# A hybrid decoder block whose down projection is computed as seven block products

## The chip, the cores and the metric

One core of a Trainium2 chip runs one launch of the kernel. The metric is the device time of that launch in microseconds (us), the median over several runs. TensorE (PE) multiplies matrices, VectorE (DVE) and ScalarE (ACT) work elementwise, GpSimd (POOL) does small elementwise work, SyncE (SP) begins the transfers. A copy engine's transfer is called a DMA here.

## What is computed

A decoder block on a sequence of 1024 tokens and 1024 channels, all float32: a Mamba-2 state scan and a differential attention side by side, merged by gates, then a gated feed-forward layer with a short causal convolution. The part that matters is the last one:

```python
u = causal_dwconv(h2 @ w_up[layer], conv_ffn_w[layer], conv_ffn_b[layer])
u_gate, u_val = jnp.split(u, 2, axis=-1)
f = (jax.nn.gelu(u_gate, approximate=True) * u_val) @ w_down[layer]
x = x + g2 * rms_norm(f, post_norm2_w[layer])
```

`w_up` is 1024 x 5632, `w_down` 2816 x 1024. The first projections of the block (`xbc` for the scan, then `z` with `dt`) and the scan itself matter too, since the change puts work beside them.

## The kernel before

Every matrix product is done on PE in a split form: each float32 operand is cut into a high and a low part (`split`: a copy on ACT for the high part, a subtraction on DVE for the low one, lines 80 to 82), and three products are summed, high x high, high x low, low x high. So one block of 128 x 128 against 512 columns costs three matmuls.

The stages in order: a first stage that normalizes x, with the first blocks of xbc and of a gate; xbc (12 blocks, with sums over rows of `w_ada` on DVE beside it); z (three column ranges of 8 token tiles each); the state scan, in which GpSimd multiplies and adds (lines 615, 616, 652, 653) and PE follows an order written by hand; q, k and gates; attention; the output products; the mix with `w_out`; up; down.

**Up** (lines 1219 to 1334) runs 22 turns over blocks of 128 channels, `fb` from 0 to 21. A turn computes a gate block and a value block together as a 2 x 2 block product in Strassen's scheme (Winograd's form): seven products instead of eight, each of 4 x 3 matmuls of 128 x 512, 84 matmuls in a turn. `order` names them: b11, b21, t2, t1, t3, b22, t4, where the right operands are blocks of h2 or sums of them. The left operands are blocks of `w_up` or sums s1 to s4 that DVE forms (line 1310). Each left operand is split into one of 12 buffers that go round (`hl_tile`): four slots of their own (`hls`) and the eight split buffers `whi` and `wlo`, which all weights share. Raw blocks of weights pass through three buffers (`wraw`). The products are accumulated in PSUM banks X, Z and Y; ACT and DVE take them out (lines 1305, 1306, 1313 to 1321) into `cg` and `cv`. X is used by four of the seven products, so that t4, for example, waits until DVE has formed `cv` from t3's sum (line 1317). Then ACT and DVE do the convolution, the gelu and the product into `ug` (lines 1325 to 1329), and SP stores `ug` to `gd` in HBM.

**Down** (lines 1336 to 1390) runs two halves of 512 tokens. For each half it loads and splits the 22 blocks of `gd` (line 1352), then runs two column halves (accumulators fx and fy). In each it loads `w_down` two blocks at a time (line 94), splits them, and does for 4 token tiles 3 matmuls per block: 2 x 2 x 22 x 4 x 3 = 1056 in all. ACT sums squares, DVE multiplies by `g2r`; after the second column half come the root (GpSimd, line 130), the scaling with the residual (line 1389) and the store.

Large tiles lie in 43 slots of 4 KB per partition (`Slots`), handed out from the front of a free list and put back at its end; all 43 are in use during up. A new tile in a slot waits until the last tile there has been read. Except in blocks under `manual_schedule`, a scheduler sets the order of each engine's instructions by its own model of when operands are ready, so an instruction may be put well ahead of its place in the text; each engine then runs its list strictly in order. Up, down and the loop over z are ordered by it; in xbc only PE's order is by hand.

Of the kernel before, what the change touches and what calls it, by code (L numbers as in the profile page):

```python
# [17 lines left out]
P = 128  # L18
# [16 lines left out]
class Slots:  # L35
# [18 lines left out]
def kernel(ctx: ExitStack, tc: tile.TileContext, a: dict, out: bass.AP, dbg=None):  # L54
# [55 lines left out]
    def new_hl(name):  # L110
        return SL.get(name, F32R, (P, 2, HALF))
# [218 lines left out]
    gd = [dp.tile([P, S], F32, tag=f"gd{i}", name=f"gd{i}") for i in range(NFF)]  # L330
# [55 lines left out]
    brow = SL.get("brow")  # L386
    n_ada, rows_done = 0, 0
# [4 lines left out]
    with tc.manual_schedule(engines={EN.PE}):  # L392
        for b in range(12):
# [46 lines left out]
    n_ev = 0  # L440
# [17 lines left out]
    SL.put(*ev)  # L458
# [761 lines left out]
    hls = [SL.get(f"hls{i}") for i in range(4)]  # L1220
# [36 lines left out]
    for fb in range(2):  # L1257
        up_first(fb)
# [35 lines left out]
    for fb in range(NFF):  # L1294
        cg, cv = cgv[fb % 2]
        e1, e2 = evs[fb % 2][:, 0, :], evs[fb % 2][:, 1, :]
        if fb >= 2:
            up_first(fb)
# [23 lines left out]
        g_ = ug[fb % 2]  # L1322
# [7 lines left out]
        SP.dma_start(gd[fb], g_)  # L1330
    SL.put(*sab, *hls, *cgv[0], *cgv[1], *evs)
    for n, _ in order:
        SL.put(*HB[n])
    SL.put(*ug, uv)

    g2r = SL.get("g2r")
    SP.dma_start(g2r, rowd[3].broadcast_to([P, D]))
    fo = [SL.get(f"fo{i}") for i in range(4)]
    x1r = [SL.get(f"x1r{i}") for i in range(4)]
    tf = SL.get("tf", F32, (P, HALF))  # L1340
    gst = [SL.get(f"gst{i}", F32, (P, 2, HALF)) for i in range(2)]
    gT = None
    ssf = const("ssf", [P, 8, 2])
    rsf = const("rsf", [P, 8])
    for half in range(2):
        if half == 1:
            SL.put(*gT)
        gT = [None] * NFF
        for fb in range(NFF):
            gT[fb] = new_hl(f"g{half}_{fb}")  # L1350
            st = gst[fb // 2 % 2][:, fb % 2, :]
            SP.dma_start(st, gd[fb][:, half * HALF : (half + 1) * HALF])
            split(gT[fb][:, 0, :], gT[fb][:, 1, :], st)
        for ch in range(2):
            if ch == 0:
                acs = [ps_wa(f"fx{half}_0"), ps_wa(f"fx{half}_1"), ps_wb(f"fx{half}_2"), ps_wc(f"fx{half}_3")]
            else:
                mmx = [ps_mm(f"fy{half}_{i}") for i in range(2)]
                acs = [mmx[i // 2][:, i % 2, :] for i in range(4)]
            last = half == 1 and ch == 1  # L1360
            wd = {}
            sched = []
            for kp in range(NFF // 2):
                if not last or kp < NFF // 2 - 3:
                    sched += [(kp, q) for q in range(4)]
            if last:
                sched += [(kp, q) for q in range(4) for kp in range(NFF // 2 - 3, NFF // 2)]
            for kp, q in sched:
                if kp not in wd:
                    wd[kp] = load_moving(a["w_down"], 2 * kp, 2, ch * HALF, HALF, f"wd{half}_{ch}_{kp}")  # L1370
                tsl = slice(q * P, (q + 1) * P)
                for kk in range(2):
                    k = 2 * kp + kk
                    wh, wl = wd[kp][0][:, kk, :], wd[kp][1][:, kk, :]
                    T.matmul(acs[q], gT[k][:, 0, tsl], wh, start=(k == 0), stop=False)  # L1375
                    T.matmul(acs[q], gT[k][:, 0, tsl], wl, start=False, stop=False)  # L1376
                    T.matmul(acs[q], gT[k][:, 1, tsl], wh, start=False, stop=(k == NFF - 1))  # L1377
            csl = slice(ch * HALF, (ch + 1) * HALF)
            for q in range(4):
                i = 4 * half + q  # L1380
                A.activation(tf, acs[q], AF.Square, accum_out=ssf[:, i, ch : ch + 1])
                V.tensor_tensor(fo[q][:, csl], acs[q], g2r[:, csl], op=ALU.mult)
                if ch == 0:
                    SP.dma_start(x1r[q], x1d[i])
                    continue
                r_ = rsf[:, i : i + 1]
                V.tensor_tensor(r_, ssf[:, i, 0:1], ssf[:, i, 1:2], op=ALU.add)
                rstd_of(r_, r_, 1.0 / D, 1e-6)
                V.scalar_tensor_tensor(fo[q], fo[q], r_, x1r[q], op0=ALU.mult, op1=ALU.add)
                SP.dma_start(out[i * P : (i + 1) * P, :], fo[q])  # L1390
# [65 lines left out]
```

## Time and profile before

| | us |
|---|---|
| median of 3 runs (1977.42 to 1981.37) | 1979.33 |
| the profiled execution, its own time | 1979.32 |
| its span | 1977.5 |

The profile records one execution. Times in it count from the start of its span. An engine's busy time is the union of its instructions; PE's matmuls overlap each other, so that the duration of one is longer than the distance to the next. A group of instructions is named by line, engine, operation, and output <- inputs, with a count, the total and mean duration, and the idle time just before them with what ended it. In a row of waits, the instruction on the left waited for the one on the right: total us, times, longest. Some records can be missing from a trace (a few per cent). The rows themselves stand in the prediction.

In the order of time the stages lie about here: first stage to 75 us, xbc to 219, z to 308, scan to 480, q, k and output of the scan to 740, attention to 1067, output and mix to 1278, up to some 1730 (down begins inside its last turn, at 1717), down to the end.

### The profile page before, as it was taken

The page shows a single profiled execution, that of the slowest core. Times are in us where ns is not written, and L with a number is a line of the kernel's source. Part 1 is how long each engine was busy: PE and PEld are TensorE (multiplying, and loading weights), DVE is VectorE, ACT ScalarE, POOL GpSimd, SP SyncE. Part 2 cuts the span into 40 slices and gives each one's busy share as a digit, 9 for nine tenths or more (in the row PEclk, how much of TensorE's full clock was granted, in tenths as well). Part 3 has the DMA queues.
Part 4 walks back from the last instruction along what each step waited for, and adds up shares of the span by engine and source line. Part 5 has one row for each costly group of instructions (what it writes and reads, how often), then busy time and mean ns, then how long its engine had stood idle before and what let it go on. Part 6 is the DMA issues. An engine that isn't in the chain of part 4 may idle for free.

```text
span 1977.5 us, 24442 instructions
## 1 busy us (share of the span) xinstructions
PE 1905.0 (96%) x9260; PEld 1579.5 (80%) x9260; DVE 1167.4 (59%) x1782; ACT 834.7 (42%) x1606; POOL 117.0 (6%) x114
## 2 busy tenths in 40 slices
PE   6999999999999999999999999979999999999997
PEld 4787998878888788888887887758888888788886
DVE  6967334565172247767666445599787777664322
ACT  5532225554232135655556322366454554543221
POOL 0000002542010000000000000000000000000000
PEclk9999999999999999999999999989999999999999
DMA  9834232235337636565623552212222222574531
GB/s 303 297 117 161 78 108 79 91 107 177 117 75 226 220 106 177 154 168 147 183 89 136 182 185 107 93 50 100 96 75 86 84 77 86 175 245 144 181 97 63
DMA packets 120414, 269.06 MB, mean 136 GB/s; under 512 B 13284, under 2 KB 44644, under 8 KB 120296
## 3 DMA queue, kind: packets, MB, share of 16 engines
q1 hardware_dynamic: 120296, 267.50, 42.5%
q8 instruction: 73, 1.20, 0.2%
q14 instruction: 45, 0.37, 0.1%
HBM read 201.37 MB, written 66.08 MB: 135 GB/s over the span
## 4 chain that ended last, share of the span: by engine, by line
PE 85%; DVE 5%; DMA 4%; ACT 3%; SPq 1%; issue 1%; POOL 0%; POOLq 0%; ACTq 0%; DVEq 0%
PE up L1247 5%; PE up L1248 5%; PE up L1249 5%; PE o L1026 3%; PE fy L1377 2%; PE fy L1376 2%; PE fy L1375 2%; PE fx L1377 2%; PE fx L1376 2%; PE fx L1375 2%; PE upy L1249 2%; PE upy L1247 2%; PE upy L1248 2%; PE xbc L103 2%; PE xbc L105 2%; PE xbc L104 2%
## 5 line engine op out<-in xcount | busy, mean ns | idle before, releaser
L1247 PE MATMUL up<-t,wu_t 128*128 128x512 f32 x264 | 107.1, 406 | 4.4 <-DVE cg L1306 3.5
L82 DVE TENSOR_TENSOR wd_lo<-wd_raw,wd_hi 128x1024 fp32r<-128x1024 f32 x44 | 53.8, 1225 | 96.6 <-ACT wd_hi L81 94.8
L1248 PE MATMUL up<-t,wu_t 128*128 128x512 f32 x264 | 104.0, 394 | 0.0
L1249 PE MATMUL up<-t,wu_t 128*128 128x512 f32 x264 | 103.4, 392 | 0.0
L1014 ACT COPY aT<-at 128x512 f32<-128x512 f32 (+2 forms) x96 | 45.9, 478 | 113.8 <-PE at L1013 113.8
L81 ACT ACTIVATE wd_hi<-wd_raw 128x1024 fp32r<-128x1024 f32 x44 | 46.6, 1059 | 96.8 <-PE fx L1377 52.9
L1026 PEld LDWEIGHTS o<-vt,aT 128*128 128x128 f32 x576 | 74.9, 191 | 10.1 <-ACT aT L1014 5.6
L1026 PE MATMUL o<-vt,aT 128*128 128x128 f32 x576 | 80.9, 277 | 1.3 <-ACT aT L1014 1.3
L81 ACT ACTIVATE wu_t<-sab 128x512 fp32r<-128x512 f32 x66 | 41.6, 632 | 79.2 <-PE up L1249 39.3
L1377 PE MATMUL fx<-wd_hi,g 128*128 128x512 f32 x176 | 68.7, 390 | 0.8 <-DVE g L82 0.7
L1247 PEld LDWEIGHTS up<-t,wu_t 128*128 128x128 f32 x264 | 49.9, 189 | 24.1 <-DVE cg L1306 9.3
L1249 PE MATMUL up<-b,wu_b 128*128 128x512 f32 x176 | 68.5, 389 | 0.0
L1376 PE MATMUL fx<-wd_lo,g 128*128 128x512 f32 x176 | 68.5, 389 | 0.0
L1375 PE MATMUL fx<-wd_hi,g 128*128 128x512 f32 x176 | 68.5, 389 | 0.0
L1248 PE MATMUL up<-b,wu_b 128*128 128x512 f32 x176 | 68.5, 389 | 0.0
L1375 PE MATMUL fy<-wd_hi,g 128*128 128x512 f32 x176 | 68.5, 389 | 0.0
L1376 PE MATMUL fy<-wd_lo,g 128*128 128x512 f32 x176 | 68.5, 389 | 0.0
L1377 PE MATMUL fy<-wd_hi,g 128*128 128x512 f32 x176 | 68.5, 389 | 0.0
L1247 PE MATMUL up<-b,wu_b 128*128 128x512 f32 x176 | 68.5, 389 | 0.0
L987 DVE TENSOR_REDUCE nmx<-sc 128x1 f32<-128x640 f32 (+3 forms) x64 | 65.6, 1024 | 2.1
L967 PE MATMUL sc<-kst,qst 128*128 128x512 f32 (+2 forms) x192 | 63.7, 340 | 0.0
L103 PE MATMUL xbc<-hT,wx_hi 128*128 128x512 f32 x160 | 63.6, 397 | 0.0
(381 smaller groups left out, 5588.5 us busy)
## 6 DMA issues: line engine op xcount, KB each, us to landing
wu_raw<-in_w_up SPq DMA_DIRECT2D x44, 512.0 KB, 3.5
wd_raw<-in_w_down SPq DMA_DIRECT2D x44, 512.0 KB, 3.7
adas<-in_w_ada SPq DMA_DIRECT2D x32, 512.0 KB, 5.7
gd<-ug SPq DMA_DIRECT2D x22, 512.0 KB, 2.7
gst<-gd SPq DMA_DIRECT2D x44, 256.0 KB, 3.5
adat<-in_w_ada SPq DMA_DIRECT2D x32, 256.0 KB, 5.9
qst<-qd SPq DMA_DIRECT2D x16, 512.0 KB, 5.0
kst<-khd SPq DMA_DIRECT2D x32, 256.0 KB, 4.9
```

The costliest lines, as they stand in the source:

```text
L81: A.activation(hi, raw, AF.Copy)
L82: V.tensor_tensor(lo, raw, hi.bitcast(F32), op=ALU.subtract)
L103: T.matmul(ps, lh, rh, start=(i == 0), stop=False)
L967: T.matmul(sc[:, n0:n1], qs_[s][:, tsl], ks_[s][:, n0:n1], start=True, stop=False)
L987: V.reduce_max(nmx[:, bq, s : s + 1], sc[:, :L], axis=AX.X, negate=True)
L1026: T.matmul(po_of[j, grp][:, qi, :], at[:, k, :], vt[j % 2][:, kt, :], start=(kt == 0), stop=(kt == i))
L1247: T.matmul(out_, wh, xh_, start=(k == 0 and not more), stop=False, skip_group_check=more)
L1248: T.matmul(out_, wh, xl_, start=False, stop=False, skip_group_check=more)
L1249: T.matmul(out_, wl, xh_, start=False, stop=(k == KH - 1), skip_group_check=more)
L1375: T.matmul(acs[q], gT[k][:, 0, tsl], wh, start=(k == 0), stop=False)
L1376: T.matmul(acs[q], gT[k][:, 0, tsl], wl, start=False, stop=False)
L1377: T.matmul(acs[q], gT[k][:, 1, tsl], wh, start=False, stop=(k == NFF - 1))
```

## The change

The down projection becomes one 2 x 2 block product in the same scheme as up. The left matrix (tokens x 2816) is cut into token halves and channel halves, the right one (`w_down`) into channel halves and column halves; a channel half is 11 blocks (`KF`).

- *Weight sums.* `down_sums(k)` loads row block k of both halves of `w_down`, forms t1 to t4 on GpSimd and stores them to HBM (`wtd`). Its transfers are begun from GpSimd's queue. Eleven calls: one after every second block of xbc (five), one at each half of a column range of z (six). Its four tiles take the last free slots (`get_last`) and are put back after z.
- *Up.* The turns alternate between the two channel halves (0, 11, 1, 12, ...). After each second turn GpSimd forms s1 to s4 from the two `ug` tiles; SP stores a11, a12, a22 and s1 to s4 to `gld` in place of `gd`. Two more slots (`gsum`) are needed, so the ring of split buffers goes from 12 to 10 and `hls` from 4 to 2.
- *Down.* Seven products (`downs`) of 11 blocks x 4 token tiles x 3 matmuls, alternately into accumulators bX and bY. Left parts of the next product are loaded and split while one runs. Sums of products are formed as in up: copies on ACT, additions on DVE into `fo`, which now has eight tiles; squares, scaling and stores follow as before.

```diff
+    def get_last(self, *args):
+        self.free_list.insert(0, self.free_list.pop())
+        return self.get(*args)
...
-    gd = [dp.tile([P, S], F32, tag=f"gd{i}", name=f"gd{i}") for i in range(NFF)]
+    KF = NFF // 2
+    gld = {n: dp.tile([P, KF, HALF], F32, tag=f"gld_{n}", name=f"gld_{n}") for n in ("a11", "a12", "a22", "s1", "s2", "s3", "s4")}
+    wtd = {n: dp.tile([P, KF, 2, HALF], F32, tag=f"wtd_{n}", name=f"wtd_{n}") for n in ("12", "34")}
...
+    wdr = [SL.get_last(f"wdr{i}", F32, (P, 2, HALF)) for i in range(2)]
+    wds = [SL.get_last(f"wds{i}", F32, (P, 2, HALF)) for i in range(2)]
+    def down_sums(k):
+        for i in range(2):
+            r0 = (k + KF * i) * P
+            G.dma_start(wdr[i].rearrange("p h c -> p (h c)"), a["w_down"][r0 : r0 + P, :])
+        (b11, b12), (b21, b22) = [(t[:, 0, :], t[:, 1, :]) for t in wdr]
+        t1, t2, t3, t4 = wds[0][:, 0, :], wds[0][:, 1, :], wds[1][:, 0, :], wds[1][:, 1, :]
+        G.tensor_tensor(t1, b12, b11, op=ALU.subtract)
+        G.tensor_tensor(t2, b22, t1, op=ALU.subtract)
+        G.tensor_tensor(t3, b22, b12, op=ALU.subtract)
+        G.tensor_tensor(t4, b21, t2, op=ALU.subtract)
+        for i in range(2):
+            G.dma_start(wtd[("12", "34")[i]][:, k, :, :], wds[i])
...
+            if b >= 2 and b % 2 == 0:
+                down_sums(b // 2 - 1)
...
+            if q == 0:
+                down_sums(n_dn)
+                n_dn += 1
...
-    SL.put(*ev)
+    SL.put(*ev, *wdr, *wds)
...
-    hls = [SL.get(f"hls{i}") for i in range(4)]
+    hls = [SL.get(f"hls{i}") for i in range(2)]
-        i = n_hl % 12
+        i = n_hl % 10
-        if i < 4:
+        if i < 2:
...
-    for fb in range(2):
+    fbs = [h * KF + k for k in range(KF) for h in range(2)]
+    for fb in fbs[:2]:
         up_first(fb)
...
+    gsum = [SL.get(f"gsum{i}", F32, (P, 2, HALF)) for i in range(2)]
+    for n_fb, fb in enumerate(fbs):
...
-        SP.dma_start(gd[fb], g_)
+        k = fb % KF
+        if fb < KF:
+            SP.dma_start(gld["a11"][:, k, :], g_[:, :HALF])
+            continue
+        SP.dma_start(gld["a12"][:, k, :], g_[:, :HALF])
+        SP.dma_start(gld["a22"][:, k, :], g_[:, HALF:])
+        (l11, l21), (l12, l22) = [(t[:, :HALF], t[:, HALF:]) for t in ug]
+        s1, s2, s3, s4 = gsum[0][:, 0, :], gsum[0][:, 1, :], gsum[1][:, 0, :], gsum[1][:, 1, :]
+        G.tensor_tensor(s1, l21, l22, op=ALU.add)
+        G.tensor_tensor(s2, s1, l11, op=ALU.subtract)
+        G.tensor_tensor(s3, l11, l21, op=ALU.subtract)
+        G.tensor_tensor(s4, l12, s2, op=ALU.subtract)
+        for n, t in (("s1", s1), ("s2", s2), ("s3", s3), ("s4", s4)):
+            SP.dma_start(gld[n][:, k, :], t)
...
+    KP = (KF + 1) // 2
+    gst = [SL.get(f"gst{i}", F32, (P, 2, HALF)) for i in range(2)]
+    gop = [[[SL.get(f"g{b}_{kp}_{n}", F32R, (P, 2, HALF)) for n in ("hi", "lo")] for kp in range(KP)] for b in range(2)]
+    es = [SL.get(f"es{i}", F32, (P, 2, HALF)) for i in range(4)]
...
+    bX = [ps_wa("dx0"), ps_wa("dx1"), ps_wb("dx2"), ps_wc("dx3")]
+    mmx = [ps_mm(f"dy{i}") for i in range(2)]
+    bY = [mmx[i // 2][:, i % 2, :] for i in range(4)]
+    downs = (("a11", "b11", bX), ("a12", "b21", bY), ("s2", "t2", bX), ("s1", "t1", bY), ("s3", "t3", bX), ("s4", "b22", bY), ("a22", "t4", bX))
+    n_st = 0
+    def left_part(p, kp):
+        nonlocal n_st
+        if p >= len(downs):
+            return
+        nk = min(2, KF - 2 * kp)
+        st = gst[n_st % 2]
+        n_st += 1
+        hi, lo = gop[p % 2][kp]
+        SP.dma_start(st[:, :nk], gld[downs[p][0]][:, 2 * kp : 2 * kp + nk, :])
+        split(hi[:, :nk], lo[:, :nk], st[:, :nk])
+    def right_part(p, kp):
+        n = downs[p][1]
+        nk = min(2, KF - 2 * kp)
+        if n[0] == "b":
+            r, c = int(n[1]) - 1, int(n[2]) - 1
+            return load_moving(a["w_down"], r * KF + 2 * kp, nk, c * HALF, HALF, f"wd{n}_{kp}")
+        raw = wp.tile([P, 2, HALF], F32, tag="wraw", name=f"wd{n}_{kp}_raw", bufs=3)
+        i = int(n[1]) - 1
+        SP.dma_start(raw[:, :nk], wtd[("12", "34")[i // 2]][:, 2 * kp : 2 * kp + nk, i % 2, :])
+        hi = wp.tile([P, 2, HALF], F32R, tag="whi", name=f"wd{n}_{kp}_hi", bufs=4)
+        lo = wp.tile([P, 2, HALF], F32R, tag="wlo", name=f"wd{n}_{kp}_lo", bufs=4)
+        split(hi[:, :nk], lo[:, :nk], raw[:, :nk])
+        return hi, lo
...
+    def finish(i, ch, src, junk):
+        csl = slice(ch * HALF, (ch + 1) * HALF)
+        o = fo[i][:, csl]
+        A.activation(junk, src, AF.Square, accum_out=ssf[:, i, ch : ch + 1])
+        V.tensor_tensor(o, src, g2r[:, csl], op=ALU.mult)
+    def write_out(i):
+        r_ = rsf[:, i : i + 1]
+        V.tensor_tensor(r_, ssf[:, i, 0:1], ssf[:, i, 1:2], op=ALU.add)
+        rstd_of(r_, r_, 1.0 / D, 1e-6)
+        V.scalar_tensor_tensor(fo[i], fo[i], r_, x1r[i % 4], op0=ALU.mult, op1=ALU.add)
+        SP.dma_start(out[i * P : (i + 1) * P, :], fo[i])
+    e_of = lambda t, q: es[2 * t + q // 2][:, q % 2, :]
+    for kp in range(KP):
+        left_part(0, kp)
+    for p, (ln, rn, bank) in enumerate(downs):
+        wd = {}
+        more = rn in ("t2", "t3", "t4", "b22")
+        last = p == len(downs) - 1
+        n_k = KP - 3 if last else KP
+        sched = [(kp, q) for kp in range(n_k) for q in range(4)] + [(kp, q) for q in range(4) for kp in range(n_k, KP)]
+        for kp, q in sched:
+            if kp not in wd:
+                wd[kp] = right_part(p, kp)
+                left_part(p + 1, kp)
+            tsl = slice(q * P, (q + 1) * P)
+            gh, gl = gop[p % 2][kp]
+            for kk in range(min(2, KF - 2 * kp)):
+                k = 2 * kp + kk
+                wh, wl = wd[kp][0][:, kk, :], wd[kp][1][:, kk, :]
+                T.matmul(bank[q], gh[:, kk, tsl], wh, start=(k == 0 and not more), stop=False, skip_group_check=more)
+                T.matmul(bank[q], gh[:, kk, tsl], wl, start=False, stop=False, skip_group_check=more)
+                T.matmul(bank[q], gl[:, kk, tsl], wh, start=False, stop=(k == KF - 1), skip_group_check=more)
+        for q in range(4):
+            if rn == "b11" or rn == "t2":
+                A.copy(e_of(0, q), bank[q])
+            elif rn == "b21":
+                V.tensor_tensor(fo[q][:, :HALF], bank[q], e_of(0, q), op=ALU.add)
+                finish(q, 0, fo[q][:, :HALF], e_of(0, q))
+                SP.dma_start(x1r[q], x1d[q])
+            elif rn == "t1":
+                A.copy(e_of(1, q), bank[q])
+            elif rn == "t3":
+                V.tensor_tensor(fo[4 + q][:, HALF:], bank[q], e_of(1, q), op=ALU.add)
+                finish(4 + q, 1, fo[4 + q][:, HALF:], e_of(1, q))
+            elif rn == "b22":
+                V.tensor_tensor(fo[q][:, HALF:], bank[q], e_of(0, q), op=ALU.add)
+                finish(q, 1, fo[q][:, HALF:], e_of(0, q))
+                write_out(q)
+                SP.dma_start(x1r[q], x1d[4 + q])
             else:
+                finish(4 + q, 0, bank[q], e_of(0, q))
+                write_out(4 + q)
```

More of the change, by code (lines that the diff above doesn't have):

```diff
@@ L1293 @@
     uv = SL.get("uv")
[L1294 to L1297, printed above, removed]
+    gsum = [SL.get(f"gsum{i}", F32, (P, 2, HALF)) for i in range(2)]
+    for n_fb, fb in enumerate(fbs):
+        cg, cv = cgv[n_fb % 2]
+        e1, e2 = evs[n_fb % 2][:, 0, :], evs[n_fb % 2][:, 1, :]
+        if n_fb >= 2:
             up_first(fb)
@@ L1332 @@
+        G.tensor_tensor(s1, l21, l22, op=ALU.add)
[4 more added lines that the diff above has]
+            SP.dma_start(gld[n][:, k, :], t)
     for n, _ in order:
         SL.put(*HB[n])
-    SL.put(*ug, uv)
+    SL.put(*sab, *hls, *cgv[0], *cgv[1], *evs, *ug, uv, *gsum)
+    KP = (KF + 1) // 2
+    gst = [SL.get(f"gst{i}", F32, (P, 2, HALF)) for i in range(2)]
@@ L1336 @@
+    gop = [[[SL.get(f"g{b}_{kp}_{n}", F32R, (P, 2, HALF)) for n in ("hi", "lo")] for kp in range(KP)] for b in range(2)]
     g2r = SL.get("g2r")
-    SP.dma_start(g2r, rowd[3].broadcast_to([P, D]))
-    fo = [SL.get(f"fo{i}") for i in range(4)]
+    es = [SL.get(f"es{i}", F32, (P, 2, HALF)) for i in range(4)]
+    fo = [SL.get(f"fo{i}") for i in range(8)]
     x1r = [SL.get(f"x1r{i}") for i in range(4)]
-    tf = SL.get("tf", F32, (P, HALF))
-    gst = [SL.get(f"gst{i}", F32, (P, 2, HALF)) for i in range(2)]
@@ L1342 @@
-    gT = None
     ssf = const("ssf", [P, 8, 2])
     rsf = const("rsf", [P, 8])
[L1345 to L1356, printed above, removed]
-            else:
[L1358 to L1390, printed above, removed]
@@ new lines @@
+    SP.dma_start(g2r, rowd[3].broadcast_to([P, D]))
+    bX = [ps_wa("dx0"), ps_wa("dx1"), ps_wb("dx2"), ps_wc("dx3")]
[13 more added lines that the diff above has]
+        split(hi[:, :nk], lo[:, :nk], st[:, :nk])
```

6 lines of the change are left out of this document (3 added, 3 removed).

## The prediction

> **What bounds the kernel now.** I read the page first: busy times, then the chain of work that ended last, then the costliest groups.
>
> ```profile
> PE 1905.0 (96%) x9260; PEld 1579.5 (80%) x9260; DVE 1167.4 (59%) x1782; ACT 834.7 (42%) x1606; POOL 117.0 (6%) x114
> PE 85%; DVE 5%; DMA 4%; ACT 3%; SPq 1%; issue 1%; POOL 0%; POOLq 0%; ACTq 0%; DVEq 0%
> L1375 PE MATMUL fx<-wd_hi,g 128*128 128x512 f32 x176 | 68.5, 389 | 0.0
> L1375 PE MATMUL fy<-wd_hi,g 128*128 128x512 f32 x176 | 68.5, 389 | 0.0
> ```
>
> TensorE (PE) is busy 96% of the span and carries 85% of the last chain. A share over the whole span does not say what the down projection is worth, so next comes the busy time by stretch (span, then busy time and count of PE, PEld, DVE, ACT, POOL, the clock, DMA share, GB/s):
>
> ```profile
> 1277.00:1320.00 43.00, 30.40 (x123) 23.10 (x122) 35.73 (x58) 21.87 (x40) 1.08 (x2) 0.80 0.10 37
> 1320.00:1700.00 380.00, 380.00 (x1658) 308.09 (x1657) 300.39 (x387) 195.65 (x284) 0.00 (x0) 1.00 0.26 88
> 1700.00:1735.00 35.00, 32.80 (x142) 25.88 (x140) 23.47 (x28) 20.04 (x27) 0.00 (x0) 1.00 0.65 213
> 1735.00:1800.00 65.00, 65.00 (x287) 53.81 (x288) 35.30 (x43) 28.90 (x43) 0.00 (x0) 1.00 0.64 213
> 1800.00:1900.00 100.00, 100.00 (x443) 82.81 (x442) 37.79 (x45) 27.33 (x36) 3.14 (x4) 1.00 0.45 156
> ```
>
> From 1735 us on, which is the down projection, PE is never idle while VectorE (DVE) and ScalarE (ACT) are busy about half the time or less. So here a removed matmul is removed time. The 389 ns of one matmul overlap with the next: the pitch is 100 us / 443 = 0.2257 us. Up (1320 to 1700) is bound by PE too, but there DVE is at 300.39/380 = 79%.
>
> **Fewer matmuls in down.** Before: lines 1375 to 1377, fx and fy, six groups of 176 = 1056 matmuls. After: 7 products x 11 column blocks x 4 token tiles x 3 = 924, of the same shape. 132 x 0.2257 = **-29.8 us**, if each product (132 matmuls, 29.8 us) stays bound by PE. Its feed, from these rows:
>
> ```profile
> L81 ACT ACTIVATE wd_hi<-wd_raw 128x1024 fp32r<-128x1024 f32 x39 | 41.3, 1059 | 96.8 <-PE fx L1377 52.9 <-PE fy L1377 43.2 <-DMA gd<-ug 0.4
> L82 DVE TENSOR_TENSOR wd_lo<-wd_raw,wd_hi 128x1024 fp32r<-128x1024 f32 x41 | 50.1, 1225 | 92.0 <-ACT wd_hi L81 90.2 <-DMA gst<-gd 1.8
> L1382 DVE TENSOR_TENSOR fo<-fx,g2r 128x512 f32<-128x512 f32 x8 | 5.5, 690 | 3.8 <-ACT tf L1381 3.8
> L1389 DVE SCALAR_TENSOR_TENSOR fo<-fo,rsf,x1r 128x1024 f32<-128x1024 f32 x4 | 5.1, 1285 | 1.8 <-POOL rsf L130 1.7
> ```
>
> A product splits 11 left and 11 right blocks of 512, that is 11 operations of 1024 width: DVE 11 x 1.225 = 13.5 us, ACT 11 x 1.059 = 11.6 us. The heaviest eviction (after b22) adds on DVE 4 x (0.69 + 0.69 + 1.285 + some 0.3 for the small ones) = 11.9 us. 25.4 us lies below 29.8. Transfers are 22 blocks of 256 KB = 5.8 MB in 29.8 us = 194 GB/s, and the old down moved 213 GB/s with PE full. The two sets of accumulators (X, Y) alternate, so each is evicted under the other's 29.8 us. The added copies and sums cost nothing there; without that cover one eviction is about 12 us. The tail (square, product, rstd, scale, store) is unchanged: 0.
>
> **Entering down.** The stretch 1700:1735 has 2.2 us without PE. The old first accumulation takes all 22 blocks, also the one that the last turn of up produces. The new first product takes a11 alone, whose last block is written one turn (19 us) before up ends, into staging whose slots come free with the last turn's first product. Between 0 and -2.2, as it can at most win what is lost; I take **-1**.
>
> **GpSimd (POOL) sums in up.** Each pair of turns gets four of 128x512. No DVE work is removed. What such a sum costs, and what it does to DVE, the state scan shows:
>
> ```profile
> 360.58 1.04 POOL L616 TENSOR_TENSOR yt<-xtk,rows 128x512 f32<-128x512 f32 x1
> 360.62 1.55 DVE L613 TENSOR_TENSOR xd<-xtk,sm 128x512 f32<-128x512 f32 x1
> 362.09 1.21 DVE L685 TENSOR_TENSOR yt<-yt,zt 128x1024 f32<-128x1024 f32 x1
> 362.31 1.89 POOL L615 TENSOR_TENSOR xdd<-xd,sm 128x512 f32<-128x512 f32 x1 [0.69 <-DVE xd L613]
> 371.29 0.68 DVE L613 TENSOR_TENSOR xd<-xtk,sm 128x512 f32<-128x512 f32 x1
> 372.12 1.04 POOL L615 TENSOR_TENSOR xdd<-xd,sm 128x512 f32<-128x512 f32 x1 [1.31 <-DVE xd L613]
> ```
>
> Alone, L613 takes 0.68 us and the POOL sum 1.04. Started 0.04 us behind a POOL sum, the same L613 takes 1.55 and ends 0.55 us after it; a POOL sum started behind a DVE product takes 1.89. They take turns; they do not run side by side. [...]
>
> So DVE loses at least 4 x 1.04 = 4.2 us per pair of turns. A turn is 84 matmuls = 19.0 us; DVE idles (380 - 300.39)/380 x 38 = 8.0 us a pair. Does the loss reach PE? These are DVE's instructions behind one turn's end, and its waits over up:
>
> ```profile
> 1673.26 1.22 DVE L1329 TENSOR_TENSOR ug<-ug,uv 128x1024 f32<-128x1024 f32 x1
> 1674.40 0.68 DVE L1306 TENSOR_TENSOR cg<-up,evs 128x512 f32<-128x512 f32 x1
> 1675.00 0.68 DVE L82 TENSOR_TENSOR wu_t<-wu_raw,wu_t 128x512 fp32r<-128x512 f32 x1
> 1679.34 0.69 DVE L82 TENSOR_TENSOR wu_b<-wu_raw,wu_b 128x512 fp32r<-128x512 f32 x1 [1.86 <-ACT wu_b L81]
> 1681.92 0.69 DVE L1317 TENSOR_TENSOR cv<-up,evs 128x512 f32<-128x512 f32 x1 [1.89 <-PE up L1249]
> DVE wu_b L82 <- ACT wu_b L81: 34.4, 17, 3.0
> DVE cv L1317 <- PE up L1249: 28.2, 18, 1.9
> PEld up L1247 <- DVE cg L1306: 4.9, 17, 0.4
> ACT wu_t L81 <- PE up L1249: 39.3, 17, 2.6
> ```
>
> The sums can start when L1329 ends, near 1674.5. L1306, the eviction on which PE waits (up to 0.4 us), reads one operand from PSUM and is already at the head. What is blocked are splits of weights, prepared products ahead: ACT waits 39.3 us for PE to give their buffers back (the last row), not the other way round. DVE then has 1.86 + 1.89 = 3.75 us of idle time before it owes the next eviction (cv), and PE does b22's product (12 x 0.2257 = 2.7 us) before it needs that one. 3.75 + 2.7 = 6.4 exceeds 4.2. Bounds: 0, and 4.2 us in each of 11 pairs = 46; a gain has no source. I take 0.2 a pair, **+2**, nearest the slack. On SP the added stores (7 a pair in place of 2) wait for POOL with the next load of up weights behind them; a few us late, that load eats into the products prepared ahead. That ring shrinks from 12 to 10 buffers, two products (5.4 us) of 12 x 2.7 = 32 us: 0.
>
> **Start of up.** The first four products had split buffers of their own; now the third and fourth use the ring that w_out still holds. The 1277:1320 stretch has 12.6 us without PE, into which they can move: 0 to 24 x 0.2257 = 5.4 us; **+1**. Evictions there can also get earlier slots; this may win back some of the 12.6, and I allow -3 for it in the range only.
>
> **Weight sums beside xbc and z.** Eleven sets, each two 512 KB loads, four sums and two 512 KB stores, all begun on POOL's own queue; SP's gets nothing in front of it. No POOL-issued transfer exists in this trace.
>
> ```profile
> 80.00:100.00 20.00, 20.00 (x90) 16.56 (x89) 16.86 (x15) 8.48 (x11) 0.00 (x0) 1.00 0.87 302
> L229 DVE TENSOR_TENSOR hT<-xh,hT x16: 681/684/693, 19.2 to 74.7; 128x512 fp32r<-128x512 f32 x16
> L455 ACT ACTIVATE ev<-z x24: 433/461/462, 219.2 to 307.4; 128x330 f32<-128x330 f32 x8, 128x346 f32<-128x346 f32 x8, 128x348 f32<-128x348 f32 x8
> 308.98 1.18 POOL L616 TENSOR_TENSOR yt<-xtk,rows 128x512 f32<-128x512 f32 x1 [279.67 <-ACT xtk L610]
> 1655.41 0.33 SPq L1330 DMA_DIRECT2D gd<-ug  x1
> 7.94 2.39 SPq L252
> wx_raw<-in_w_xbc SPq DMA_DIRECT2D x10, 512.0 KB, 5.4
> ```
>
> An issue lies between 0.33 and 2.39 us (SP's shortest and a long one), a landing near 5.4, four sums between 4.2 and 4 x 1.89 = 7.6. A set then takes 4 x 0.33 + 5.4 + 4.2 = 10.9 to 4 x 2.39 + 5.4 + 7.6 = 22.6 us; in between, 15. [...] Their slots come free at about 75 us (L229) and POOL is next needed at 309 (L616). The sets depend on nothing else, so I expect them early: 11 x 15 = 165, done by 240. DVE is at 84% in 80:100 and DMA at 302 GB/s, so some work moves later; PE keeps three raw blocks ahead. Bounds 0 to +5; **+1**.
>
> **Sum.** -29.8 - 1 + 2 + 1 + 1 = -26.8. On the profiled run's span of 1977.5 us: 1950.7. Its own time is 1979.32, 1.8 us above its span, and equals the median of the three (1979.33). Forecast **1952.5 us**. Its own range: 1979.3 - 29.8 - 2.2 - 3 = 1944 to about 1963 (waits of 1 us a pair in up).
>
> **Rivals.** *The lock reaches PE.* For it: DVE would go from 79% to 90% in up. Against it: the 6.4 us of slack. In a mild form, 2 us a pair, 22 in place of 2: 1972. In full, 4.2 a pair, 46 in place of 2: **1996**, slower. It decides from 26.8 + 2 = 28.8 us on, 2.6 us in each of the 11 pairs.
>
> *POOL is late for the scan.* If the sets run where they stand, the six in z begin at 219. At 22.6 us a set they end at 355, 46 us after POOL is due; the scan stands still: 1952.5 + 46 = 1998. At 15 us they end at 309 and cost nothing. Against it: nothing holds the sets back.
>
> *Down does not speed up*: feeding or a changed order stretches each product to 33 us, 7 x 3.2 = 22 us: about 1975. For it only the 25.4 us of DVE in one product.
>
> **How the numbers follow.** Forecast 0.77, lock mild 0.09, lock full 0.05, late POOL 0.05, no speed-up 0.04. A change within 0.2% (4 us) can't be told from none. Faster: 0.77 + 0.09 = 0.86; same 0.04; slower 0.10. To hold 8 in 10 the range goes from 1944 through most of the mild lock: 1974.
>
> **What would show it.** Right: 924 matmuls at 0.226 us and PE full through down (some 209 us); up's turns at 19.0 us; the last weight sum before 300 us. Wrong: waits of PE for cv or cg by 2 us and more after every second turn; POOL busy with weight sums past 309; PE idle between products of down.

## The result and the profile after

| | us |
|---|---|
| before, median of 4 runs (1977.42 to 1981.37) | 1979.47 |
| after, median of 4 runs (1956.17 to 1965.86) | 1962.78 |
| ratio, 95% interval | 0.9911, 0.9884 to 0.9939 |
| the profiled execution after, its own time / its span | 1963.24 / 1961.5 |

The change makes the kernel faster by 16.7 us, 0.9%. The forecast was 26.8 us, 1952.5; the time lies 10 us above it. The busy times of the page after:

```profile
PE 1880.9 (96%) x9128; PEld 1556.9 (79%) x9128; DVE 1237.0 (63%) x1790; ACT 844.8 (43%) x1614; POOL 277.1 (14%) x246
```

PE has 132 matmuls less, but its busy time fell by 24.1 us, not by 29.8, and DVE's rose by 69.6 us. Where the missing time is shows when the starts of the stages are set side by side (the first matmul into each stage's accumulators; us from the start of the span):

| | before | after | later by |
|---|---|---|---|
| z | 214.6 | 226.8 | +12.2 |
| scan | 307.3 | 319.7 | +12.4 |
| attention | 713.6 | 724.0 | +10.4 |
| up | 1278.1 | 1289.8 | +11.7 |
| last matmul of down starts | 1967.0 | 1953.6 | -13.4 |
| end of the span | 1977.5 | 1961.5 | -16.0 |

So the delay arises before z, in the first 227 us: 12.2 us, all in the stage xbc. From the first matmul of up to the last of down it takes 689 us before and 664 after, -25.1. The end behind the last matmul is 2.6 us shorter. This sums to -15.5; the middle stages give 0.5 more.

**Down.** The window over the whole down projection after (span, then busy time and count of PE, PEld, DVE, ACT, POOL, clock, DMA share, GB/s):

```profile
1743.00:1954.00 211.00, 210.22 (x926) 173.27 (x924) 120.28 (x132) 90.50 (x123) 13.18 (x10) 1.00 0.64 212
```

PE is full: 924 matmuls at 0.2257 are 208.6, and the first and the last of them start 210.4 us apart. The seven products follow each other without a gap; the only wait shown is 0.8 us inside the third one, for one of its split blocks (`wdt_lo`). That is as forecast.

**xbc.** The same 140 us before and after:

```profile
75.00:215.00 140.00, 139.76 (x602) 112.51 (x601) 96.15 (x86) 44.65 (x46) 0.00 (x0) 1.00 0.48 160
```

```profile
75.00:215.00 140.00, 130.94 (x551) 104.66 (x550) 104.38 (x80) 40.05 (x41) 74.25 (x73) 0.98 0.79 284
```

Before, PE was full here and DVE busy for 96 of 140 us. After, PE stands idle for 9.1 us, 8.8 more than before, and has a granted clock of 0.98, which by an estimate is another 2.8 us in 140: together 11.6 of the 12.2 us by which z is late. What PE waited for:

```profile
PE xbc L107 <- DVE cu L433: 8.8, 4, 6.8
```

The `cu` operations are DVE's three steps of the convolution that read an xbc block out of its PSUM bank. DVE is busy for 8.2 us more although it finished fewer instructions (80 in place of 86). Its groups by form say which ones grew. First before:

```profile
L370 DVE SCALAR_TENSOR_TENSOR accr<-adas,scl,accr 128x1024 f32<-128x1024 f32 x21 | 26.9, 1283 | 3.1 <-DMA adas<-in_w_ada 2.6
L408 DVE SCALAR_TENSOR_TENSOR cu<-xbc,vec,cu 128x1023 f32<-128x1023 f32 x12 | 15.3, 1279 | 0.5 <-ACT cu L406 0.4
L82 DVE TENSOR_TENSOR wx_lo<-wx_raw,wx_hi 128x1024 fp32r<-128x1024 f32 x10 | 12.1, 1223 | 22.3 <-ACT wx_hi L81 22.3
```

and after:

```profile
L378 DVE SCALAR_TENSOR_TENSOR accr<-adas,scl,accr 128x1024 f32<-128x1024 f32 x21 | 33.6, 1601 | 7.9 <-DMA adas<-in_w_ada 7.5
L86 DVE TENSOR_TENSOR wx_lo<-wx_raw,wx_hi 128x1024 fp32r<-128x1024 f32 x10 | 16.4, 1654 | 14.1 <-ACT wx_hi L85 14.1
L433 DVE SCALAR_TENSOR_TENSOR cu<-xbc,vec,cu 128x1023 f32<-128x1023 f32 x11 | 13.9, 1274 | 0.2 <-ACT cu L431 0.2
```

`accr` and `wx_lo` read two operands from SBUF: their means grew from 1283 to 1601 and from 1223 to 1654 ns. `cu` is the same operation as `accr` on almost as many elements, but one of its operands (`xbc`) lies in PSUM: 1279 and 1274, unchanged. Of these groups, the ones with two SBUF operands are held up by GpSimd's sums, by 318 and 431 ns an operation, and the one with an operand in PSUM is not. This holding up of DVE by GpSimd is called the lock from here on; the prediction means by it the product of 1.55 us beside a sum, in place of 0.68. The second loss is in the idle column: in front of `accr`, DVE waited 7.5 us in place of 2.6 for blocks of `w_ada`, whose loads now share the DMA engines with the weight sets (0.79 busy in place of 0.48).

How it reaches PE is to be seen at its longest gap; DVE's, GpSimd's and PE's instructions after, with their start, duration and idle time before:

```profile
177.80 1.28 DVE L378 SCALAR_TENSOR_TENSOR accr<-adas,scl,accr 128x1024 f32<-128x1024 f32 x1 [2.70 <-DMA adas<-in_w_ada]
179.00 2.32 DVE L86 TENSOR_TENSOR wgs_lo<-wgs_raw,wgs_hi 128x1024 fp32r<-128x1024 f32 x1
181.24 1.27 DVE L433 SCALAR_TENSOR_TENSOR cu<-xbc,vec,cu 128x1023 f32<-128x1023 f32 x1
...
184.82 2.31 DVE L378 SCALAR_TENSOR_TENSOR accr<-adas,scl,accr 128x1024 f32<-128x1024 f32 x1
187.05 1.27 DVE L433 SCALAR_TENSOR_TENSOR cu<-xbc,vec,cu 128x1021 f32<-128x1021 f32 x1
```

```profile
178.59 1.64 POOL L405 TENSOR_TENSOR wds<-wdr 128x512 f32<-128x512 f32 x1 [7.92 <-DMA wdr<-in_w_down]
181.27 1.27 POOL L406 TENSOR_TENSOR wds<-wdr,wds 128x512 f32<-128x512 f32 x1 [1.04 <-DMA wdr<-in_w_down]
...
184.79 1.26 POOL L408 TENSOR_TENSOR wds<-wdr,wds 128x512 f32<-128x512 f32 x1
```

```profile
181.24 0.39 PE L109 MATMUL xbc<-hT,wx_lo 128*128 128x512 f32 x1
188.47 0.76 PE L107 MATMUL xbc<-hT,wx_hi 128*128 128x512 f32 x1 [6.84 <-DVE cu L433]
```

PE needs the three `cu` operations before it may write the bank again. They stand in DVE's list among the sums over `w_ada`, and DVE did not take them ahead of it: ACT had done its step of `cu` at 172.72 (L431, 1.19 us from 171.53), and the first of the three began at 181.24. What held them up is a wait of 2.70 us for a load, then `wgs_lo` and one `accr` stretched by 1.1 and 1.0 us, each beside a GpSimd sum. The `accr` at 184.82 began 0.03 us behind a sum of 1.26 us and ended 1.08 us behind it: it stood still until the sum was done. The `cu` at 181.24 ran beside a sum, both at their full speed of 1.27. PE idles for 6.84 us and then begins slowly, at a clock of 0.66 in the stretch with the gap:

```profile
185.00:195.00 10.00, 6.53 (x18) 5.18 (x19) 8.78 (x7) 2.82 (x3) 4.45 (x6) 0.66 0.70 246
```

**Up.** DVE's two most affected groups over up, before and after, and GpSimd's sums:

```profile
L82 DVE TENSOR_TENSOR wu_t<-sab,wu_t 128x512 fp32r<-128x512 f32 x66 | 45.3, 689 | 0.0
L1310 DVE TENSOR_TENSOR sab<-wu_raw 128x512 f32<-128x512 f32 x44 | 30.0, 689 | 1.6 <-DMA wu_raw<-in_w_up 1.1
```

```profile
L86 DVE TENSOR_TENSOR wu_t<-sab,wu_t 128x512 fp32r<-128x512 f32 x66 | 58.1, 885 | 2.4 <-ACT wu_t L85 2.4
L1343 DVE TENSOR_TENSOR sab<-wu_raw 128x512 f32<-128x512 f32 x44 | 46.8, 1098 | 2.0 <-DMA wu_raw<-in_w_up 2.0
L1371 POOL TENSOR_TENSOR gsum<-ug,ug 128x512 f32<-128x512 f32 x10 | 12.9, 1286 | 171.0 <-DVE ug L1362 157.2 <-issue 13.8
L1373 POOL TENSOR_TENSOR gsum<-ug 128x512 f32<-128x512 f32 x11 | 18.2, 1658 | 202.1 <-DVE ug L1362 202.1
```

The lock costs DVE 12.8 + 16.8 = 29.6 us here, 2.7 in each of the 11 pairs of turns. PE's loading waited for `cg` 14.3 us in place of 9.3 over up and down:

```profile
PEld up L1247 <- DVE cg L1306: 9.3, 19, 3.3
```

```profile
PEld up L1278 <- DVE cg L1339: 14.3, 21, 3.3
```

Most of the stretch stayed in the slack, as forecast.

### The profile page after: what moved, and what is told of

Same layout as the page of the kernel before. It is cut to its first block, busy times and chain, and to the rows that moved or that the text cites. A ratio compares the mean times of both kernels' runs of the same rounds, so it can differ in the third digit from the quotient of the medians.

```text
span 1961.5 us, 24609 instructions
## 1 busy us (share of the span) xinstructions
PE 1880.9 (96%) x9128; PEld 1556.9 (79%) x9128; DVE 1237.0 (63%) x1790; ACT 844.8 (43%) x1614; POOL 277.1 (14%) x246
## 5 line engine op out<-in xcount | busy, mean ns | idle before, releaser
L86 DVE TENSOR_TENSOR g_lo<-gst,g_hi 128x1024 fp32r<-128x1024 f32 (+1 forms) x42 | 49.3, 1179 | 57.1 <-ACT g_hi L85 55.6
L134 POOL TENSOR_TENSOR sqt<-sqt,nhalf 128x4 f32<-128x4 f32 x16 | 16.1, 1008 | 481.0 <-DVE sqt L133 414.9
L85 ACT ACTIVATE g_hi<-gst 128x1024 fp32r<-128x1024 f32 (+1 forms) x42 | 41.3, 988 | 76.3 <-DMA gst<-gld_s 33.1
L107 PE MATMUL xbc<-hT,wx_hi 128*128 128x512 f32 x160 | 64.5, 403 | 8.8 <-DVE cu L433 8.8
L1278 PEld LDWEIGHTS up<-t,wu_t 128*128 128x128 f32 x264 | 50.0, 189 | 27.8 <-DVE cg L1339 14.3
L1018 DVE TENSOR_REDUCE nmx<-sc 128x1 f32<-128x640 f32 (+3 forms) x64 | 65.6, 1024 | 2.1
L1360 DVE SCALAR_TENSOR_TENSOR ug<-cg,vec,ug 128x1023 f32<-128x1023 f32 (+1 forms) x44 | 56.5, 1283 | 14.4 <-ACT ug L1358 13.7
L109 PE MATMUL xbc<-hT,wx_lo 128*128 128x512 f32 x160 | 63.3, 395 | 0.0
L108 PE MATMUL xbc<-hT,wx_hi 128*128 128x512 f32 x160 | 63.2, 395 | 0.0
L999 PE MATMUL sc<-klo,qst 128*128 128x512 f32 (+2 forms) x192 | 63.0, 345 | 0.0
L107 PE MATMUL z<-wz_hi,hT 128*128 128x346 f32 (+1 forms) x192 | 61.8, 323 | 0.1
L108 PE MATMUL z<-wz_lo,hT 128*128 128x346 f32 (+1 forms) x192 | 61.8, 322 | 0.0
```

Source lines behind the costliest of these rows:

```text
L86: V.tensor_tensor(lo, raw, hi.bitcast(F32), op=ALU.subtract)
L107: T.matmul(ps, lh, rh, start=(i == 0), stop=False)
L108: T.matmul(ps, lh, rl, start=False, stop=False)
L109: T.matmul(ps, ll, rh, start=False, stop=(i == n - 1))
L999: T.matmul(sc[:, n0:n1], qs_[s][:, tsl], kl[s][:, n0:n1], start=False, stop=True)
L1018: V.reduce_max(nmx[:, bq, s : s + 1], sc[:, :L], axis=AX.X, negate=True)
```

## The experiments

The runs below the first of the table stand in three groups, each on one chip with the kernel before beside it: without sums, without transfers, no sets and no sums in up (before: 1980.15 us); beside z and gates, up's sums on DVE, both, and by SP (1978.58); the last three and the change again (1978.51). "Sets" are the eleven weight sets of `down_sums`. Ratios to the kernel before, with their intervals:

| run | us | ratio | z starts at | up, first matmul to first of down |
|---|---|---|---|---|
| the change | 1962.78 | 0.9911 (0.9884 to 0.9939) | 226.8 | 453.4 |
| the change again | 1959.16 | 0.9909 (0.9893 to 0.9925) | 225.3 | 453.4 |
| sets without sums | 1954.62 | 0.9874 (0.9856 to 0.9891) | 219.5 | 453.5 |
| sets without transfers | 1962.40 | 0.9913 (0.9898 to 0.9928) | 226.3 | 452.7 |
| no sets | 1950.57 | 0.9855 (0.9831 to 0.9880) | 214.0 | 452.0 |
| no sums in up | 1956.84 | 0.9887 (0.9872 to 0.9902) | 227.9 | 450.2 |
| sets beside z and gates | 1958.74 | 0.9902 (0.9883 to 0.9922) | 214.8 | 452.9 |
| sums in up on DVE | 1957.56 | 0.9894 (0.9875 to 0.9912) | 221.8 | 450.7 |
| both of these | 1956.32 | 0.9885 (0.9869 to 0.9902) | 216.1 | 450.8 |
| set transfers begun by SP | 1957.15 | 0.9894 (0.9879 to 0.9908) | 220.8 | 452.5 |
| sets beside gates and attention output | 1970.46 | 0.9960 (0.9947 to 0.9972) | 214.0 | 453.7 |
| the same, sums in up on DVE | 1969.19 | 0.9947 (0.9936 to 0.9959) | 215.3 | 449.7 |
| weight sums on DVE | 1965.42 | 0.9936 (0.9919 to 0.9953) | 229.1 | 453.5 |

**What in the sets costs the time?** First the sums alone are taken out, then the transfers alone, then both.

```diff
...
-        G.tensor_tensor(t1, b12, b11, op=ALU.subtract)
...
-            G.dma_start(wtd[("12", "34")[i]][:, k, :, :], wds[i])
+            G.dma_start(wtd[("12", "34")[i]][:, k, :, :], wdr[i])
...
```

This one leaves the weight sums out: what is stored is the loaded blocks.

> The changed kernel without the four GpSimd sums of each set beside xbc and z: the loaded rows of w_down are stored as they are, so the weight sums are left out and all POOL transfers stay. The changed kernel loses some 12 us in xbc (first matmul of z at 226.8 us, 214.6 before the change). Theory 'lock': DVE is held up by POOL's sums and evicts xbc late; then z starts near 215 and the time is about 1951 us. Theory 'transfers': POOL's 23 MB delay the loads of w_ada and w_xbc, and DVE stands waiting for them; then z starts at 224 or later and the time stays at 1961 to 1963. If both are needed, z starts near 219, 1955.

In the next, only the first two sets are loaded and stored whole, the others in 16 of 1024 columns, and down reads the first two throughout; all sums are formed.

```diff
+            n = HALF if k < 2 else 8
-            G.dma_start(wdr[i].rearrange("p h c -> p (h c)"), a["w_down"][r0 : r0 + P, :])
+            G.dma_start(wdr[i][:, :, :n], a["w_down"][r0 : r0 + P, :].rearrange("p (h c) -> p h c", h=2)[:, :, :n])
...
```

> The changed kernel with all weight sums on GpSimd, but from the third set on only 16 of 1024 columns are loaded and stored, so POOL's transfers shrink from 23 MB to about 4.5 MB; down reads the first two sets again and again, so most weight sums are left out of the result. Theory 'lock': z starts at 222 or later, time about 1960 us, since the same 44 sums run beside xbc. Theory 'transfers': z starts near 215, time about 1951.

The third has no sets at all; where down takes a sum, it loads a plain block of `w_down`, and the four slots stay held back.

```diff
     def down_sums(k):
-        for i in range(2):
...
+        pass
...
```

> The changed kernel without the sets beside xbc and z; down loads blocks of w_down in place of the weight sums, which are left out. The same slots are held back, so nothing else moves. Both theories: z starts within 1 us of 214.6 and the time is 1950 to 1952 us, which is the forecast without its term for xbc. If the 12 us came from the slots that were taken from the end of the free list, z stays near 226 and the time at 1962.

z starts 4.9 us later than before with the transfers alone, 11.7 later with the sums alone, 12.2 with both, and 0.6 earlier with neither. The two do not add up. With neither, the slots are still held back, so they are not what costs the time. The same DVE group in the first and in the second run:

```profile
L378 DVE SCALAR_TENSOR_TENSOR accr<-adas,scl,accr 128x1024 f32<-128x1024 f32 x21 | 26.9, 1283 | 8.2 <-DMA adas<-in_w_ada 7.9
```

```profile
L378 DVE SCALAR_TENSOR_TENSOR accr<-adas,scl,accr 128x1024 f32<-128x1024 f32 x21 | 36.4, 1733 | 5.9 <-DMA adas<-in_w_ada 5.4
```

Without sums the operation is as short as before and only the waits for loads are left; without the transfers it is longer than in the changed kernel, since sums that wait less for loads come closer together in xbc (in the 140 us GpSimd is busy for 94.93 us in place of 74.25). So the lock is the larger part, and it would cost nearly the whole by itself. The times say the same: without sums 1954.62, without transfers 1962.40, in intervals that do not overlap. How much the transfers cost alone is less sure. The four profiles with the same code up to z (the change twice, no sums in up, and sums in up on DVE) have z start anywhere between 221.8 and 227.9, so 4.9 us from one profile is a rough figure, and the times without sums and without sets have overlapping intervals. Without the sets the time is 1950.57 (four runs from 1946.92 to 1954.73): with their term of +1 struck out, the forecast sum is 1951.5. That they agree so closely is in part luck, since 2.6 us were gained at the end of the kernel that are not in the sum.

**What do GpSimd's sums in up cost?** The sums in up are left out; halves of `ug` are stored in their place.

```diff
-        G.tensor_tensor(s1, l21, l22, op=ALU.add)
...
-        for n, t in (("s1", s1), ("s2", s2), ("s3", s3), ("s4", s4)):
+        for n, t in (("s1", l11), ("s2", l21), ("s3", l12), ("s4", l22)):
...
```

> The changed kernel without GpSimd's four sums after each second turn of up: the four halves of ug are stored in their place, so s1 to s4 are left out, with the same number of stores. Theory 'slack' (the prediction): the lock costs up 2 us or less, time 1960 to 1963 us. Theory 'lock reaches PE in up': 5 us or more come back, 1958 or less, and PE's waits for cg shrink from 14.3 us to the 9.3 us of before.

Then they are kept, but formed on DVE:

```diff
-        G.tensor_tensor(s1, l21, l22, op=ALU.add)
+        V.tensor_tensor(s1, l21, l22, op=ALU.add)
...
```

> The changed kernel, complete, with the four sums after each second turn of up on DVE in place of POOL. A DVE sum of this size holds DVE some 0.6 us, a POOL sum holds it up 1.29 us. Theory 'lock': DVE gains, 4 x 0.6 = 2.4 us of work a pair against 4 x 1.29 = 5.2 us of waiting; up shortens by 1 to 4 us, time 1958 to 1961. Rival 'DVE has no room': the sums stand in DVE's queue ahead of the next evictions, PE's waits for cg grow above 14.3 us, time 1964 or more.

Up takes 452.0 to 453.7 us in the nine profiles with the sums on GpSimd, 450.2 without them and 449.7 to 450.8 in the three with the sums on DVE. So GpSimd's sums cost up about 3 us and DVE's nothing that shows. That lies between the two theories of the first run (2 us or less, 5 or more); PE's loading waited 11.3 us for `cg` there, in place of 14.3 with the sums and 9.3 before. DVE's groups with the sums on DVE say why:

```profile
L1343 DVE TENSOR_TENSOR sab<-wu_raw 128x512 f32<-128x512 f32 x44 | 29.6, 683 | 1.0 <-DMA wu_raw<-in_w_up 1.0
L1373 DVE TENSOR_TENSOR gsum<-ug 128x512 f32<-128x512 f32 x11 | 7.5, 681 | 0.0
L1371 DVE TENSOR_TENSOR gsum<-ug,ug 128x512 f32<-128x512 f32 x10 | 6.8, 681 | 0.0
```

44 sums of 0.68 us are 30 us of DVE, and nothing is stretched; on GpSimd the same sums took 29.6 us from it by the lock, 0.67 us a sum and not the expected 1.29. The 3 us are read from the length of up in the profiles: the times of the changed kernel measured again (0.9909), without the sums (0.9887) and with them on DVE (0.9894) can't be told apart.

**Can the sets stand elsewhere?** Six are put beside z, five beside the gates after the scan; then the same with up's sums on DVE.

```diff
-            if b >= 2 and b % 2 == 0:
-                down_sums(b // 2 - 1)
...
     for j in range(3, 8):
+        down_sums(j + 3, wdr, wds)
         w = load_block(a["w_gate"][j], f"wgs{j}")
...
```

> The changed kernel, complete, with the weight sums moved out of xbc: six sets beside z, in slots that come free only at the end of xbc, and five beside the gate blocks after the scan. Theory (lock plus transfers, both only in xbc's crowded DVE queue): z starts near 214.6 us, z and the gates keep their length because DVE is idle most of the time there, and the time is 1950 to 1953 us, as without the sets. If sets cost wherever they stand, z takes more than its 92 us or the scan starts late, and the time stays at 1957 or more.

> The changed kernel, complete, with the sets moved out of xbc and the sums of up on DVE. If the two costs are separate, their gains add: 1946 to 1950 us. If the second is nothing, 1950 to 1953.

A miss for both: xbc gets its 12 us back, but z now takes 100 us and more in place of 92, and the times are 1958.74 and 1956.32. Waits around z in the first of the two:

```profile
ACT wz_hi L85 <- DMA wz_raw<-in_w_zdt: 6.3, 2, 4.8
...
PE z L107 <- ACT wz_hi L85: 4.9, 1, 4.9
```

The blocks of z's next column range come late beside the sets' transfers. Whether the transfers or the slots delay them was not tested. Next the sets are put beside the gates (five) and the attention output (six), where DVE has more room.

```diff
...
+        if j < 6:
+            down_sums(j + 5, wdr, wds)
         w = load_block(a["w_attn_o"][j], f"wao{j}")
...
```

> The eleven sets of weight sums are taken out of xbc and z; five stand beside the gate blocks after the scan, six beside the blocks of w_attn_o after attention. Theory (the sets cost where DVE and the loads of the stage beside them are tight, as beside xbc and z): z starts at 214 to 215 us and takes 92 us as before the change, and the stages beside which the sets now stand take no more than 2 us longer, so the time is 1950 to 1953 us. Rival (a set costs about 1 us wherever it stands, as the 11 sets in xbc did and the six beside z did again): z starts at 214, but the gates and the attention output together give back 8 to 12 us, and the time stays at 1958 to 1963.

> As the run before, and the four sums of each pair of turns in up on DVE (4 x 0.68 us) in place of GpSimd. Theory (in up GpSimd's sums cost DVE more than they take off it): another 2 to 4 us less than with the sums on GpSimd, 1947 to 1950 us, up 450 to 451 us in place of 453.4. Rival (the 3 us in up come from the added stores and loads, not from who sums): the same as the run before within 1 us.

One half came out: beside the gates the sets are free, but the times are 1970.46 and 1969.19. The stretch with the gates, before and then in the first of the two:

```profile
480.00:710.00 230.00, 226.58 (x1027) 186.32 (x1027) 76.83 (x82) 46.99 (x63) 11.58 (x6) 0.99 0.54 161
```

```profile
480.00:710.00 230.00, 226.70 (x1028) 186.21 (x1028) 78.44 (x82) 47.34 (x63) 47.60 (x44) 1.00 0.65 206
```

GpSimd works 36 us more, and PE and DVE do not notice: here five sets cost nothing. But from the first matmul of attention to the first of up it took 564.5 us before and 585.6 here. SyncE's queue, with the wait that ends it, and DVE's next instruction:

```profile
1148.99 0.38 SPq L98 DMA_DIRECT2D wo_raw<-in_w_out  x1
1175.51 0.32 SPq L1195 DMA_DIRECT2D g1r<-rowd  x1
1175.93 0.37 SPq L1169 DMA_DIRECT2D gth<-gad  x1
```

```profile
SPq L1195 <- DMA wdrc<-in_w_down: 22.1, 1, 22.1
SPq L1195 <- POOL wdsc L406: 3.9, 1, 3.9
```

```profile
1183.88 1.28 DVE L1175 SCALAR_TENSOR_TENSOR mt<-gth,ao 128x512 f32<-128x512 f32 x2 [25.03 <-DMA gth<-gad]
```

The load of `g1r` for the next stage got a slot that the last set had held, and stood in SyncE's queue for 26 us until that set was done (22.1 for its loads, 3.9 for its sums); the loads of `gth`, which the running stage needed, stood behind it. DVE waited 25 us for them, PE 9.6. From 1070 to 1200 us PE stood idle for 13.6 of 130 us at a granted clock of 0.93; before, from 1070 to 1185, for 3.4 of 115 at 1.00. The wait of 25 us is a price of the slots and the queue in this placing, not of GpSimd's work; the rest of the 21 us was not traced to a cause. Other slots for the two sides were not tried. With up's sums on DVE as well, up is 4.0 us shorter (449.7 in place of 453.7), as its theory has it, but the two times can't be told apart.

**Who should begin the transfers, who form the weight sums?** SyncE begins the sets' transfers in place of GpSimd:

```diff
...
-            G.dma_start(wtd[("12", "34")[i]][:, k, :, :], wds[i])
+            SP.dma_start(wtd[("12", "34")[i]][:, k, :, :], wds[i])
```

> The changed kernel, complete, with the transfers of the weight sums begun by SP in place of POOL. The sums stay beside xbc, so the lock stays: z not before 224 under 'lock'. SP's queue is in order, so loads of w_ada and w_xbc may stand behind a store that waits for POOL: then xbc gets longer still, z at 230 or later and 1967 us or more. If SP's queue has room, 1960 to 1964.

A miss: it is not slower. z starts at 220.8, 4.5 and 6.0 us earlier than in the two profiles of the change; but the kernel with up's sums on DVE, which has the same code up to z as the change, has it at 221.8. A difference of this size can't be read from one profile, and the ratios overlap. `accr` is stretched here too (1553 ns), so the lock is there although z starts before the 224 that was set for it. Then DVE forms the weight sums:

```diff
-        G.tensor_tensor(t1, b12, b11, op=ALU.subtract)
+        V.tensor_tensor(t1, b12, b11, op=ALU.subtract)
...
```

> The weight sums stay where the change puts them, their transfers still begun by GpSimd, but DVE forms them (4 x 0.68 = 2.7 us a set). Theory (a GpSimd sum holds up DVE's operations with two SBUF inputs for all of its own time, 1.3 to 2.3 us): DVE does the same work in half the time that it lost, z starts at 219 to 224 us in place of 222 to 228, time 1955 to 1959. Rival (DVE works strictly in order, and a sum that waits for its load holds back the eviction behind it, on which PE waits): z starts at 230 us or later and the time is 1965 or more.

> The changed kernel once more, on the chip of the three runs before, so that they can be compared with it: 1956 to 1964 us, z starting at 222 to 228 us.

The first theory fell: z starts at 229.1 and the time is 1965.42. What the rival describes is to be seen, but its interval (0.9919 to 0.9953) overlaps that of the change measured again, so that DVE is the worse place here isn't shown by the times. DVE's groups in xbc:

```profile
L378 DVE SCALAR_TENSOR_TENSOR accr<-adas,scl,accr 128x1024 f32<-128x1024 f32 x21 | 26.8, 1277 | 5.5 <-DMA adas<-in_w_ada 5.4
...
L405 DVE TENSOR_TENSOR wds<-wdr 128x512 f32<-128x512 f32 x9 | 6.2, 691 | 14.2 <-DMA wdr<-in_w_down 9.1 <-DMA wtd<-wds 5.1
L406 DVE TENSOR_TENSOR wds<-wdr,wds 128x512 f32<-128x512 f32 x9 | 6.2, 687 | 6.8 <-DMA wdr<-in_w_down 6.8
```

The lock is gone (1277 ns), the sums take 0.69 us each, and z still starts no earlier: DVE now stands still for 14.2 + 6.8 us before sums whose blocks have not come (9.1 and 6.8) or whose tile is still being stored (5.1), with the evictions behind them. On GpSimd no eviction stands behind such a wait. In up, where the operands are DVE's own `ug`, nothing is waited for, and DVE was the better place.

No complete version is clearly faster than the change: the best, 0.9885, overlaps with 0.9909 measured again.

## Why the forecast was right, and where it was off

The time lies at the upper edge of the forecast's own range, 1944 to about 1963. That edge was drawn for waits in up, and the loss came in xbc; that the range still held it is luck. In the two profiles the sum of -26.8 became -16.0: 11.2 us more for the sets, 2.7 more from the first matmul of up to the last of down, 2.6 less at the tail and 0.5 less in between.

- *Fewer matmuls in down, -29.8, and entering it, -1.* Held. Seven products at PE's pitch, no gap between them; from up's first to down's last matmul -25.1, with up's terms in it (forecast -27.8). From the last matmul of up to the last of down it takes 210.6 us in place of 240.1, -29.5. Up, from its first matmul to its last, takes 453.2 in place of 448.8, +4.4, where the forecast had +3.
- *Start of up, +1.* Held. The first 43 us have 13.7 us without PE in place of 12.6:

```profile
1289.00:1332.00 43.00, 29.31 (x116) 22.45 (x115) 36.54 (x61) 21.84 (x40) 1.10 (x2) 0.76 0.11 37
```

- *GpSimd's sums in up, +2.* Held: about 3. The lock took 2.7 us of DVE per pair, not the assumed 4.2 or more, and it fell on weight splits ahead of PE, as argued (that the eviction L1306, with an operand in PSUM, goes on beside a sum had no row in the prediction; after, as L1339, it took 0.69 us at 1361.77 beside a sum that began at 1361.99, and 684 ns in the mean in place of 685); the waits for `cg` grew by 5 us of PE's loading. The mild and the full form of the rival, 22 and 46 us, didn't occur.
- *Weight sums beside xbc and z, +1 within 0 to +5.* **This term was mis-sized: it measured +12.** The step that failed is "some work moves later; PE keeps three raw blocks ahead". The lock had been read from the scan and was weighed for up, where DVE is 79% busy, but it was not applied to xbc, where DVE was at 84% in 80:100 by the quoted row. There are no three blocks of slack on the side that counts: PE waited not for weights but for its PSUM bank, that is for the three `cu` operations in DVE's ordered list, among operations that GpSimd stretches and that wait for loads. The length of a set was about right: eleven of them took from 71 to 241 us, where the prediction had 15 us each and an end at 240. So the sums of ten sets ran before z began, and what the term lacked was their price for DVE. A sum of two full operands also takes GpSimd 1.29 us alone (the `gsum` row of L1371); the quoted 1.04 was for one with a broadcast operand. The 0.33 us called SP's shortest issue is not the shortest in that trace (0.23 at 217.41); GpSimd's own issues took 0.56 at the median for stores. Neither changes the term.
- *The tail, 0.* It became 2.6 us shorter. Before, the last token tiles ended in pairs and two were still to be evicted behind the last matmul (ACT's squares at 1967.47 and 1968.92); after, they end one by one, 3.4 us apart, and one is left. Both programs write the last matmuls token tile by token tile; what differs there is that two token tiles of `fy` share one PSUM tile, while each of `dx` has its own. That this is the cause was not tested.

```profile
1967.47 0.60 ACT L1381 ACTIVATE tf<-fy 128x512 f32<-128x512 f32 x1 [6.09 <-PE fy L1377]
1968.92 0.60 ACT L1381 ACTIVATE tf<-fy 128x512 f32<-128x512 f32 x1 [0.76 <-DVE fo L1382]
```

```profile
1954.11 0.60 ACT L1426 ACTIVATE es<-dx 128x512 f32<-128x512 f32 x1 [2.71 <-PE dx L1456]
```

- *GpSimd late for the scan.* Didn't occur: the last two stores of a set were issued at 239.7 and 240.3 us, before the forecast's mark of 300.

## What to carry to other kernels

Work put on an engine that stands idle is free only if the stage beside it has room on everything that this work shares: here the SBUF operands of DVE, the DMA engines, the slots and the queues. Price it in each stage in which it stands, by the operations that the bottleneck waits for, not only in the stage that the change is about: five sets cost nothing beside the gates and twelve us came with the ones that stood beside xbc. A GpSimd sum can take as much from a DVE that is busy with two SBUF operands as forming it there would (29.6 of 30 us in up), so nothing is gained by it where the data is at hand. Where the sum has to wait for its data, DVE stood still for 21 us before it, with other work behind; no time shows which engine is the better one then.

## What was not expected of the hardware

- How exactly the lock follows the operands: beside GpSimd's sums `accr` (two SBUF operands) went from 1283 to 1601 ns, `cu` (one in PSUM, the same operation on 1023 in place of 1024 elements) from 1279 to 1274.
- After PE's gap of 6.84 us the granted clock was 0.66 over the ten us around its end, and the first matmuls were 0.56 and 0.43 us apart in place of 0.2257 (starts at 188.47, 189.03, 189.46). The 13 matmuls up to 193.98 took 5.5 us in place of 13 x 0.2257 = 2.9, and from there on the distance is about 0.23 again. So this gap cost some 2.6 us more than its length.
- The same code up to z had z start at 227.9, 226.8, 225.3 and 221.8 us in four profiles (no sums in up, the change, the change again, sums in up on DVE). PE waited for `cu` for 8.8 us in the change, 7.2 in the change again and 3.5 with up's sums on DVE. In the first two of these `accr` took 1601 and 1636 ns, and DVE's wait for its blocks of `w_ada` was 7.5 and 7.8 us; these two rows don't tell the loads from the lock as what makes the spread.
